# Gates of a gated block in pairs by Strassen's seven half-size products, with low parts of weights by an adding DMA

## The chip, the cores and the metric

The kernel runs on one core of one Trainium2 chip. The metric is the device time of one execution in microseconds (us), lower is better. Engines are named as in the profile: PE (TensorE, matmuls), PEld (its weight loads), DVE (VectorE), ACT (ScalarE), POOL (GpSimd) and SP (the engine that issues most DMAs).

## The reference

One layer over 512 tokens of width 1024, in float32. Of it, these lines matter:

```python
h = rmsnorm(x, norm_mix_pre[l])
(c_q, c_kv, k_r, sg_u, sg_v, cv_x, cv_b, cv_c, pool_in, gate_pre) = split_cols(h @ w_in[l])
gates = jax.nn.sigmoid(gate_pre + gate_b[l]).reshape(B_, S_, N_BRANCH, D_)
y_a = mla(...) @ w_br_mla[l]            # attention branch, (512, 256) @ (256, 1024)
y_b = spatial_gating(...) @ w_br_sg[l]
y_c = short_conv(...) @ w_br_conv[l]
y_d = multiscale_pool(...) @ w_br_pool[l]
merged = (gates[:, :, 0] * y_a + gates[:, :, 1] * y_b
          + gates[:, :, 2] * y_c + gates[:, :, 3] * y_d)
x = x + rmsnorm(merged @ w_out[l], norm_mix_post[l])
h = rmsnorm(x, norm_ffn_pre[l])
f = jnp.square(jax.nn.relu(h @ w_ff1[l])) @ w_ff2[l]     # d_ff = 4096
x = x + rmsnorm(f, norm_ffn_post[l])
```

The four gates are 4 x 1024 columns of `w_in`, so `gate_pre` alone is a product of 512 x 1024 by 1024 x 4096.

## The kernel before

**Three matmuls for one.** Every large product is made from operands split in two: a high part (the value rounded to the format float32r, written by a cast on ACT) and a low part (the value less its high part, written by a subtraction on DVE). `mm3` (line 125) multiplies high by high, high by low and low by high into one PSUM bank. All matmuls go through the wrapper at line 95, so the profile shows L95 for all of PE and ACT; they are told apart by their tiles.

**Weights.** `load` (line 110) brings a tile of 128 x 1024 (512 KB) from HBM into one of three `raw` buffers by a DMA on SP. `split_w` (line 115) casts it to `wh` on ACT and subtracts to `wl` on DVE. `wh` and `wl` have five buffers each. A buffer is written again only when the last matmul that reads it has ended.

**Gates and merge.** The columns are worked in eight blocks b of 128. For each block, `gate(b, i)` (line 439) makes the four gates i = 0 to 3: 24 matmuls (8 K tiles by 3) of 512 columns with the normalized input z, split as `zh` and `zl`, into a bank `fb`; then DVE multiplies the bank by `rbc` into a tile `g`. `merge(b)` (line 447) applies the sigmoid on ACT, loads one tile of branch weights (`wB`), makes four products `y` of 6 matmuls each with the branch results `aT` to `dT`, multiplies each by its gate on DVE, adds them up and splits the sum into `mh` and `ml`. Block 0's gates are made as filler between the steps of attention; the others follow in a loop (lines 669 to 672).

**Output product and feed-forward.** `wo` multiplies the merged tiles by `w_out`, in two halves of columns; each row tile is normalized, added to x (`x1`), transposed (`turn_h`, tiles `tr`) and split into `hh` and `hl`. The first feed-forward product (tiles `z`) starts early for the first four of its 32 hidden row tiles: the lower half of the token columns first (256 columns, line 757), the upper half when the last row tile is there (line 818). The other 28 are made in pairs j, j + 1 by Strassen's scheme (lines 845 to 885): four sums of the quarter weights on DVE, three sums of the halves of h (`hsum`, made once), and seven products `part` of 12 matmuls of 256 columns (4 K tiles by 3) into banks pa to pd, combined by copies on ACT and adds on DVE. `second()` (line 797) makes one K tile of the second product, 12 matmuls of 512 columns into four banks `acc`, from a hidden tile u that `usplit` has split into `uh` and `ul`.

**What sets the order.** PE keeps the program's order. The other engines' instructions are placed by a scheduler when the program is built, and each engine then runs its list strictly in order; waits are semaphores. SP issues its DMAs in order too, each when its buffer is free.

Of the kernel before, what the change touches and what calls it, by code (L numbers as in the profile page):

```python
# [10 lines left out]
F32 = mybir.dt.float32  # L11
# [69 lines left out]
def build(ctx, tc, d, out):  # L81
# [22 lines left out]
    def f(t):  # L104
        return t.bitcast(F32)
# [339 lines left out]
    gates = []  # L445

    def merge(b):
        for i, g in enumerate(gates):
            ACT.activation(g, g, AF.Sigmoid, bias=k1("gateb")[:, i * 8 + b:i * 8 + b + 1])
        w = weights(d["wB"][b])  # L450
        prev = None
        for i, br in ((1, bT), (2, cT), (3, dT), (0, aT)):
            g = gates[i]
# [8 lines left out]
        ACT.copy(mh[:, b, :], prev)  # L462
        DVE.tensor_tensor(ml[:, b, :], prev, f(mh)[:, b, :], ALU.subtract)
        gates.clear()

    others = branches()

# [188 lines left out]
    right = dict(side="right")  # L656

    TOP = 20
    xp = ctx.enter_context(tc.tile_pool(name="xp", bufs=1, reuse_waits="tile", **right))
    x1 = xp.tile([P, NT, D], F32, name="x1")  # L660
    r2 = xp.tile([P, TOP], F32, name="r2")[:, :NT]
    mp = ctx.enter_context(ExitStack())
    mpool = mp.enter_context(tc.tile_pool(name="mp", bufs=1, reuse_waits="tile", **right))
    mh = mpool.tile([P, KD, S], F32R, name="mh")
    ml = mpool.tile([P, KD, S], F32R, name="ml")
    mT = (mh, ml)
    gmix = mpool.tile([P, D], F32, name="gmix")
    gffn = mpool.tile([P, D], F32, name="gffn")
# [4 lines left out]
    nc.sync.dma_start(gmix, d["gmix"].partition_broadcast(P))  # L673
    nc.sync.dma_start(gffn, d["gffn"].partition_broadcast(P))
    for t in range(NT):
        nc.sync.dma_start(x1[:, t, :], d["x"][t * P:(t + 1) * P, :])
    s1.close()

    HK, HS = KD // 2, S // 2
    hs = ExitStack()
    hp_ = hs.enter_context(tc.tile_pool(name="hp", bufs=1, reuse_waits="tile"))

# [41 lines left out]
    for hf in range(2):  # L731
        wo = [weights(d["wO"][hf, c]) for c in range(4)]
        for t in range(NT):
            ps = bank("wo")
            for k in range(KD):
                mm3(ps, sl(mT, slice(None), k, slice(t * P, (t + 1) * P)),
                    sl(wo[k // 2], slice(None), slice((k % 2) * 512, (k % 2 + 1) * 512)), k == 0, k == KD - 1)
# [40 lines left out]
    sst = up.tile([P, 64], F32, name="sst")[:, :4 * NT].rearrange("p (t c) -> p t c", c=4)  # L778
# [50 lines left out]
    A11, A12, A22, S4 = (sl(h2, slice(None), k, t) for k, t in  # L829
                         ((slice(0, HK), slice(0, HS)), (slice(HK, KD), slice(0, HS)), (slice(HK, KD), slice(HS, S)),  # L830
                          (slice(0, HK), slice(HS, S))))
    S1, S2, S3 = (sl(hsum, slice(None), c) for c in range(3))
    fx = hs.enter_context(tc.tile_pool(name="fx", bufs=1, reuse_waits="tile"))
    B1, B2 = slice(0, 512), slice(512, 1024)

    def small():
        return fx.tile([P, HS], F32, tag="x", name="x", bufs=5)

    def part(ps, w, at, a, first):

        for k in range(HK):
            mm3(ps[:, :HS], sl(w, slice(None), slice(at + k * P, at + (k + 1) * P)), sl(a, slice(None), k),
                first and k == 0, k == HK - 1, not first)

    for j in range(EARLY, NFF, 2):
        g, h = u[j], u[j + 1]
        left, rght = load(d["w1"][j]), load(d["w1"][j + 1])
        w = split_w(left)
        w22 = split_w(rght[:, B2], 512)

        DVE.tensor_tensor(left[:, B1], rght[:, B1], left[:, B1], ALU.subtract)
        DVE.tensor_tensor(rght[:, B1], rght[:, B2], rght[:, B1], ALU.subtract)
        DVE.tensor_tensor(rght[:, B2], rght[:, B2], left[:, B1], ALU.subtract)
        DVE.tensor_tensor(left[:, B2], left[:, B2], rght[:, B2], ALU.subtract)
        wl = split_w(left)
        wr = split_w(rght)
        pa, pb = bank("pa"), bank("pb")
        part(pa, w, 0, A11, True)
        x1_ = small()
        ACT.copy(x1_, pa[:, :HS])  # L860
        part(pb, w, 512, A12, True)
        DVE.tensor_tensor(g[:, :HS], pb[:, :HS], x1_, ALU.add)
        pc = bank("pc")
        part(pc, wl, 0, S1, True)
        x5 = small()
        ACT.copy(x5, pc[:, :HS])
        part(pa, wr, 512, S2, False)
        x2 = small()
        ACT.copy(x2, pa[:, :HS])
        pd = bank("pd")  # L870
        part(pd, wl, 512, A22, True)
        second()
        part(pc, w22, 0, S4, False)
        DVE.tensor_tensor(h[:, :HS], pc[:, :HS], x2, ALU.add)
        part(pa, wr, 0, S3, False)
        x3 = small()
        ACT.copy(x3, pa[:, :HS])
        DVE.tensor_tensor(g[:, HS:], pd[:, :HS], x3, ALU.add)  # L878
        DVE.tensor_tensor(h[:, HS:], x3, x5, ALU.add)
# [131 lines left out]
```

## Time and profile before

| | us |
|---|---|
| median of 3 runs (lowest, highest) | 747.95 (746.12, 748.18) |
| the profiled execution: its time | 746.96 |
| the profiled execution: its span in the trace | 745.3 |
| PE busy in the span | 729.6 |
| DVE busy | 470.9 |
| ACT busy | 353.1 |
| POOL busy | 13.3 |

The span is the time from the first to the last traced event of one execution; 1.7 us of the execution's time lie outside it. Matmuls are pipelined: the profile gives one of 512 columns 0.39 us, but the next starts 0.227 us behind it. So a duration of a run of matmuls is read from the chain of work in order of time, which counts from start to start, and not from the busy time of one.

### The profile page before, as it was taken

The numbers are of one execution on the slowest core, as the hardware profiler recorded it, in microseconds if no ns is written. First come the engines' busy times: TensorE is split into PE (matmuls) and PEld (weight loads), VectorE is DVE, ScalarE is ACT, GpSimd is POOL, SyncE is SP. The second block draws the span as 40 slices with busy tenths as digits, with TensorE's granted clock in tenths as the row PEclk, the third lists the DMA queues.
The fourth block names the chain that finished last, engine by engine and source line by source line (L and its number), as shares of the span: only waits on it lengthen the run. The fifth ranks groups of instructions, "written<-read, shape, count | busy, mean of one in ns | idle before, by whom it ended". The sixth has DMA issues, their size and how long they took to land.

```text
span 745.3 us, 10302 instructions
## 1 busy us (share of the span) xinstructions
PE 729.6 (98%) x4058; PEld 637.9 (86%) x4058; DVE 470.9 (63%) x764; ACT 353.1 (47%) x580; POOL 13.3 (2%) x28
## 2 busy tenths in 40 slices
PE   9999999999999999999999699999999999999996
PEld 8988888888888888888889599999999999888885
DVE  7599975366365355455369667776677776774424
ACT  6875543533232323323346356555565556753411
POOL 1110000000000000000000000000000000000001
PEclk9999999999999999999999899999999999999999
DMA  8523231452323223232213014232333233533203
GB/s 306 199 88 114 85 113 58 139 201 85 113 85 98 100 92 107 85 113 86 80 34 113 29 60 142 86 110 86 118 109 111 88 92 133 172 113 104 67 0 113
DMA packets 23152, 78.77 MB, mean 106 GB/s; under 512 B 3008, under 2 KB 3520, under 8 KB 23104
## 3 DMA queue, kind: packets, MB, share of 16 engines
q1 hardware_dynamic: 23072, 78.12, 31.7%
q8 instruction: 32, 0.52, 0.3%
q14 instruction: 16, 0.13, 0.1%
q0 software_dynamic: 32, 0.00, 0.0%
HBM read 76.01 MB, written 2.10 MB: 105 GB/s over the span
## 4 chain that ended last, share of the span: by engine, by line
PE 88%; DVE 8%; ACT 2%; issue 1%; DMA 0%; POOL 0%; SPq 0%; DVEq 0%; ACTq 0%
PE fb L95 26%; PE acc L95 24%; PE pa L95 8%; PE wo L95 6%; PE y L95 6%; PE pc L95 5%; PE psA L95 3%; PE pd L95 3%; PE pb L95 2%; PE z L95 2%; PE sgv L95 2%; DVE wl L119 1%; PE po L95 1%; DVE ql L539 1%; DVE kl L539 1%
## 5 line engine op out<-in xcount | busy, mean ns | idle before, releaser
L95 ACT CAST wh<-raw 128x1024 fp32r<-128x1024 f32 (+2 forms) x154 | 153.9, 1009 | 233.6 <-issue 105.4
L119 DVE TENSOR_TENSOR wl<-raw,wh 128x1024 fp32r<-128x1024 f32 (+2 forms) x154 | 178.7, 1169 | 34.4 <-ACT wh L95 32.3
L95 PE MATMUL fb<-zh,wh 128*128 128x512 f32 x336 | 131.4, 391 | 0.1
L95 PE MATMUL fb<-zh,wl 128*128 128x512 f32 x336 | 130.8, 389 | 0.0
L95 PE MATMUL fb<-zl,wh 128*128 128x512 f32 x336 | 130.8, 389 | 0.0
L95 PE MATMUL acc<-wh,uh 128*128 128x512 f32 x232 | 91.5, 394 | 3.6 <-ACT uh L95 3.6
L95 PE MATMUL acc<-wh,ul 128*128 128x512 f32 x232 | 91.3, 394 | 3.5 <-DVE ul L788 3.5
L95 PE MATMUL acc<-wl,uh 128*128 128x512 f32 x232 | 91.4, 394 | 0.0
L442 DVE TENSOR_TENSOR g<-fb,rbc 128x512 f32<-128x512 f32 x32 | 22.1, 692 | 96.7 <-PE fb L95 96.7
L788 DVE TENSOR_TENSOR ul<-u,uh 128x512 fp32r<-128x512 f32 x58 | 38.7, 690 | 57.3 <-ACT uh L95 57.3
L95 PEld LDWEIGHTS fb<-zh,wl 128*128 128x128 f32 x336 | 63.1, 188 | 13.3
L95 PEld LDWEIGHTS fb<-zh,wh 128*128 128x128 f32 x336 | 63.1, 188 | 13.2 <-DVE zc L351 0.4
L95 PEld LDWEIGHTS fb<-zl,wh 128*128 128x128 f32 x336 | 63.1, 188 | 12.7
L95 PEld LDWEIGHTS acc<-wh,ul 128*128 128x128 f32 x232 | 44.1, 190 | 13.7 <-DVE ul L788 4.3
L95 PEld LDWEIGHTS acc<-wh,uh 128*128 128x128 f32 x232 | 44.0, 190 | 12.5 <-ACT uh L95 4.2
L95 PEld LDWEIGHTS acc<-wl,uh 128*128 128x128 f32 x232 | 44.0, 190 | 8.1
L95 ACT CAST uh<-u 128x512 fp32r<-128x512 f32 x58 | 34.3, 619 | 33.9 <-PE acc L95 33.7
L95 ACT ACTIVATE u<-u 128x512 f32<-128x512 f32 x60 | 33.2, 623 | 15.8 <-DVE u L878 15.8
L95 PE MATMUL pa<-hsh,wh 128*128 128x256 f32 x112 | 31.3, 280 | 0.3 <-ACT x L95 0.3
L95 PE MATMUL pa<-hsl,wh 128*128 128x256 f32 x112 | 31.2, 279 | 0.0
L95 PE MATMUL pa<-hsh,wl 128*128 128x256 f32 x112 | 31.2, 279 | 0.0
L95 PE MATMUL wo<-wh,mh 128*128 128x512 f32 x64 | 25.1, 392 | 0.0
(311 smaller groups left out, 1412.8 us busy)
## 6 DMA issues: line engine op xcount, KB each, us to landing
raw<-in_w SPq DMA_DIRECT2D x64, 512.0 KB, 3.5
raw<-in_wG SPq DMA_DIRECT2D x32, 512.0 KB, 3.4
raw<-in_wF SPq DMA_DIRECT2D x10, 512.0 KB, 3.5
raw<-in_wB SPq DMA_DIRECT2D x8, 512.0 KB, 3.4
raw<-in_wO SPq DMA_DIRECT2D x8, 512.0 KB, 3.4
xk<-in_x SPq DMA_DIRECT2D x4, 512.0 KB, 8.8
x<-in_x SPq DMA_DIRECT2D x4, 512.0 KB, 5.9
out<-f SPq DMA_DIRECT2D x8, 256.0 KB, 2.0
```

The source lines that it names most:

```text
L95: ins = op(*a, **k)
L119: DVE.tensor_tensor(lo[:, :n], raw[:, :n], f(hi)[:, :n], ALU.subtract)
L442: DVE.tensor_tensor(g, ps, rbc, ALU.mult)
L539: DVE.tensor_tensor(dst[1][rows, :], src, f(dst[0])[rows, :], ALU.subtract)
L788: DVE.tensor_tensor(ul, u[j], f(uh), ALU.subtract)
```

## The change

1. **Blocks 2 to 7.** The gates are made in pairs (0, 1) and (2, 3), each by `seven`, the code that was in the feed-forward loop, now a generator. z takes the place of h: three sums of its quarters (`zsum`) are made once while the gates of blocks 0 and 1 run, and a quarter of `zh` and `zl` is overwritten with a fourth sum. The results are multiplied by `rbc` in SBUF.
2. **The merge** is a generator too. The merge of block b - 1 is put into the first pair of block b, one product y behind each of the parts 2, 3, 5 and 6. Block 7's merge stands alone.
3. **`split_by_dma`** makes the low part without DVE: ACT writes the high part, then its negative into `wl`, and a DMA on POOL's queue adds the raw weights from HBM to it. It is used for the raw parts of the gate pairs (w and w22), for all merges and for the first four feed-forward tiles. The sums of weights (wl and wr) are still split by `split_w`.
4. **`second()`** is first called behind the upper halves of all four early tiles (it was called behind the second), and once more inside the first pair.
5. **Memory.** The merged tiles are single tiles in two pools. x1, gmix and gffn are allocated, and their loads issued, behind the merges.

```diff
+    def split_by_dma(src, raw=None, n=1024):
+        raw = load(src, n) if raw is None else raw
+        hi = wp.tile([P, 1024], F32R, tag="wh", name="wh", bufs=5)
+        lo = wp.tile([P, 1024], F32R, tag="wl", name="wl", bufs=5)
+        ACT.copy(hi[:, :n], raw[:, :n])
+        ACT.activation(lo[:, :n], f(hi)[:, :n], AF.Copy, scale=-1.0)
+        POOL.dma_start(lo[:, :n], src.bitcast(F32R), accum_op=ALU.add)
         return hi, lo
...
+    def seven(srcs, forms, small, g, h, by_dma):
+        A11, A12, A22, S1, S2, S3, S4 = forms
+        left, rght = load(srcs[0]), load(srcs[1])
+        if by_dma:
+            w = split_by_dma(srcs[0], left)
+            w22 = split_by_dma(srcs[1][:, B2], rght[:, B2], 512)
+        else:
+            w = split_w(left)
+            w22 = split_w(rght[:, B2], 512)
+        DVE.tensor_tensor(left[:, B1], rght[:, B1], left[:, B1], ALU.subtract)
...
+        wl = split_w(left)
+        wr = split_w(rght)
+        pa, pb = bank("pa"), bank("pb")
+        part(pa, w, 0, A11, True)
+        x1 = small()
+        ACT.copy(x1, pa[:, :HS])
+        yield
+        part(pb, w, 512, A12, True)
+        DVE.tensor_tensor(g[:, :HS], pb[:, :HS], x1, ALU.add)
+        yield
...
     def merge(b):
-        for i, g in enumerate(gates):
+        gs = list(gates)
+        gates.clear()
+        for i, g in enumerate(gs):
             ACT.activation(g, g, AF.Sigmoid, bias=k1("gateb")[:, i * 8 + b:i * 8 + b + 1])
-        w = weights(d["wB"][b])
+        w = split_by_dma(d["wB"][b])
...
+            yield
...
-    for b in range(KD):
-        while len(gates) < 4:
-            gates.append(gate(b, len(gates)))
-        merge(b)
...
+    ops = forms(z, zsum)
+    for b in range(2, KD):
+        steps = merge(b - 1)
+        for i in (0, 2):
+            g, h = (gp.tile([P, S], F32, tag="g", name="g", bufs=6) for _ in range(2))
+            for n, _ in enumerate(seven((d["wG"][4 * b + i], d["wG"][4 * b + i + 1]), ops, small_g, g, h, True)):
+                if i == 0 and n in (1, 2, 4, 5):
+                    next(steps)
+                if i == 0 and n == 5:
+                    rest(steps)
+            for x in (g, h):
+                DVE.tensor_tensor(x, x, rbc, ALU.mult)
+            gates.extend((g, h))
+    rest(merge(KD - 1))
...
-        w, ps = weights(d["w1"][j]), bank("z")
+        w, ps = split_by_dma(d["w1"][j]), bank("z")
...
+        if j == EARLY - 1:
+            second()
         pend.append((j, usplit(j)))
-        if j:
-            second()
```

In the rows of the order below, a number behind a name tells one buffer's use from the next, a bracket names the semaphores that the instruction waits for (DMASW are DMAs of POOL's queue, DMAHW those of SP's), and L95 is the wrapper's line.

ACT, the cast of a merge's weights. Before, in block 1 (wh_2197 is the merge's, the others are gates' weights, g the sigmoids):

```order
L95 CAST wh_2127<-raw_2125 128x1024 [waits DMAHW2_49,PE_49,Activation_49]
L95 ACTIVATE g_1977<-g_1977,c1_109 128x512 [waits DVE_49]
L95 CAST wh_2160<-raw_2158 128x1024 [waits DMAHW3_49,PE_49,Activation_49]
L95 ACTIVATE g_2010<-g_2010,c1_109 128x512 [waits DVE_49]
L95 CAST wh_2197<-raw_2195 128x1024 [waits DMAHW4_49,PE_49,Activation_49]
```

Now, where block 3 begins (wh_2217 and wh_2221 are the sums of its first pair, wh_2260 the merge's of block 2; pa_2095 is the last product of block 2's second pair, pa_2225 the first of block 3):

```order
L95 CAST wh_2217<-raw_2199 128x1024 [waits DVE_49,PE_49]
L95 CAST wh_2221<-raw_2201 128x1024 [waits PE_49]
L95 CAST wh_2260<-raw_2258 128x1024 [waits DMAHW3_49,PE_49]
L95 COPY x_2191<-pa_2095 128x256 [waits PE_49]
L95 ACTIVATE wl_2261<-wh_2260 128x1024 [waits DMASW4_49,Activation_49]
L95 COPY x_2239<-pa_2225 128x256 [waits PE_49]
```

The cast of wh_2197 waited for the last product y of the merge before; that of wh_2260 waits for the last matmul but one of pa_2095, the last that reads the high part of the sums of the pair before. Behind it now stand a copy, the negated copy, and on POOL the adding DMA.

PE, the first product y of a merge. Before, in block 1, behind the last gate (fb):

```order
L95 MATMUL fb_2164<-zl_105,wh_2160 128x512
L95 MATMUL fb_2164<-zh_104,wl_2161 128x512
L95 MATMUL y_2201<-bh_112,wh_2197 128x512 [waits DVE_49,Activation_49]
L95 MATMUL y_2201<-bl_113,wh_2197 128x512
L95 MATMUL y_2201<-bh_112,wl_2198 128x512 [waits DVE_49]
```

Now, in block 3, behind the second part (pb) of its first pair:

```order
L95 MATMUL pb_2226<-zl_105,wh_2203 128x256
L95 MATMUL pb_2226<-zh_104,wl_2204 128x256
L95 MATMUL y_2265<-ah_110,wh_2260 128x512 [waits Activation_49]
L95 MATMUL y_2265<-al_111,wh_2260 128x512
L95 MATMUL y_2265<-ah_110,wl_2261 128x512 [waits DMASW1_49]
```

The third matmul of the merge waited for DVE's subtraction and now waits for a DMA of POOL's queue, 24 matmuls of 256 columns and two of 512 behind the end of the pair before.

PE, the first K tile of the second product (acc). Before, it stands behind the upper half of early tile 1:

```order
L95 MATMUL z_3373<-hl_2968,wh_3369 128x256
L95 MATMUL z_3373<-hh_2967,wl_3370 128x256
L95 MATMUL acc_3531<-wh_3603,uh_3567 128x512 [waits PE_49,Activation_49]
L95 MATMUL acc_3531<-wl_3604,uh_3567 128x512
L95 MATMUL acc_3531<-wh_3603,ul_3568 128x512 [waits DVE_49]
```

Now behind that of early tile 3:

```order
L95 MATMUL z_4298<-hl_3799,wh_4293 128x256
L95 MATMUL z_4298<-hh_3798,wl_4294 128x256
L95 MATMUL acc_4375<-wh_4503,uh_4411 128x512 [waits PE_49,Activation_49]
L95 MATMUL acc_4375<-wl_4504,uh_4411 128x512
L95 MATMUL acc_4375<-wh_4503,ul_4412 128x512 [waits DVE_49]
```

Two more upper halves, 48 matmuls, stand ahead of it. And on ACT, ahead of them, the negated copies of early tiles 2 and 3 (wh_4241, wh_4293) stand behind work on the last row tiles of the output product:

```order
L95 CAST hh_3798<-tr2_4156 128x4x128 [waits PE_49]
L95 ACTIVATE sq_4165,stt_3814<-x1_3792 128x1024 [waits DVE_49,Activation_49,Pool_49]
L95 COPY lower_3815<-tr2_4149 128x4x128 [waits DVE_49]
L95 COPY lower_3815<-tr2_4156 128x4x128 [waits DVE_49]
L95 ACTIVATE wl_4242<-wh_4241 128x1024 [waits DMASW6_49]
L95 ACTIVATE sq_4287,stt_3814<-x1_3792 128x1024 [waits DVE_49,DMAHW5_49,Activation_49,Pool_49]
L95 ACTIVATE wl_4294<-wh_4293 128x1024 [waits DMASW4_49]
```

Before, no such copy was there: the low parts were subtractions in DVE's list, behind the same copies' sources.

## Rows read from the trace of the kernel before

**Rows 1.** The page's busy times, and its chain by engine (shares of span).

```profile
PE 729.6 (98%) x4058; PEld 637.9 (86%) x4058; DVE 470.9 (63%) x764; ACT 353.1 (47%) x580; POOL 13.3 (2%) x28
...
PE 88%; DVE 8%; ACT 2%; issue 1%; DMA 0%; POOL 0%; SPq 0%; DVEq 0%; ACTq 0%
```

**Rows 2.** Chain in time, one block: start us, duration us, engine, tile, matmuls.

```profile
183.26 21.76 PE fb L95 x96
205.02 5.44 PE y L95 x24
```

**Rows 3.** The same chain in the first feed-forward product, part of one pair.

```profile
520.71 2.75 PE acc L95 x12
523.46 1.40 PE pa L95 x12
```

**Rows 4.** Stretches: length; busy of PE, PEld, DVE, ACT, POOL; clock; DMA share, GB/s.

```profile
178.00:341.00 163.00, 163.00 (x721) 134.97 (x720) 84.14 (x102) 50.09 (x61) 0.00 (x0) 1.00 0.30 97
```

**Rows 5.** Groups on ACT and DVE by shape: busy us, mean ns | idle before.

```profile
L95 ACT CAST wh<-raw 128x1024 fp32r<-128x1024 f32 x138 | 144.1, 1053 | 211.7 <-issue 105.4 <-PE pc L95 42.1 <-PE fb L95 40.6
L95 ACT COPY x<-pa 128x256 f32<-128x256 f32 x42 | 15.5, 369 | 4.3 <-PE pa L95 3.2
L119 DVE TENSOR_TENSOR wl<-raw,wh 128x1024 fp32r<-128x1024 f32 x138 | 167.7, 1223 | 27.3 <-ACT wh L95 25.3 <-issue 0.3
L852 DVE TENSOR_TENSOR raw<-raw 128x512 f32<-128x512 f32 x14 | 9.7, 692 | 0.5
L862 DVE TENSOR_TENSOR u<-pb,x 128x256 f32<-128x256 f32 x14 | 5.9, 420 | 2.1 <-PE pb L95 2.1
```

**Rows 6.** DMA issues: tile, queue, count, KB each, median us to landing.

```profile
raw<-in_wB SPq DMA_DIRECT2D x8, 512.0 KB, 3.4
x<-in_x SPq DMA_DIRECT2D x4, 512.0 KB, 5.9
gmix<-in_gmix SPq DMA_DIRECT2D x1, 512.0 KB, 4.9
gffn<-in_gffn SPq DMA_DIRECT2D x1, 512.0 KB, 5.8
pos<-in_pos POOLq DMA_DIRECT2D x1, 2.0 KB, 2.6
```

**Rows 7.** Chain in time, start of the feed-forward.

```profile
392.67 8.49 PE z L95 x72
401.15 0.45 PE tr L95 x4
...
417.58 0.61 DVE ul L788
...
433.82 1.40 PE pa L95 x12
```

**Rows 8.** PE in time there: start, duration, [idle before, its releaser].

```profile
414.04 0.50 PE L95 MATMUL acc<-wh,uh 128*128 128x512 f32 x1 [3.60 <-ACT uh L95]
...
418.24 0.80 PE L95 MATMUL acc<-wh,ul 128*128 128x512 f32 x1 [3.47 <-DVE ul L788]
```

**Rows 9.** Stretches there; the number behind POOL's is the granted clock.

```profile
415.00:416.00 1.00, 0.00 (x0) 0.00 (x0) 1.00 (x3) 0.00 (x0) 0.00 (x0) 0.76 0.00 0
420.00:422.00 2.00, 2.00 (x6) 1.52 (x6) 0.12 (x1) 0.00 (x0) 0.00 (x0) 0.50 0.00 0
422.00:424.00 2.00, 2.00 (x16) 1.86 (x15) 0.00 (x0) 0.00 (x0) 0.00 (x0) 0.91 0.00 0
```

**Rows 10.** Stretches at the end of the kernel.

```profile
738.00:740.00 2.00, 0.85 (x4) 0.38 (x2) 0.24 (x2) 0.78 (x2) 0.00 (x0) 1.00 0.70 262
742.00:744.00 2.00, 0.00 (x0) 0.00 (x0) 0.05 (x1) 0.00 (x0) 0.00 (x0) 0.80 0.70 262
```

**Rows 11.** ACT in time, end of the output product.

```profile
395.05 1.19 ACT L95 COPY lower<-tr 128x512 f32<-128x512 f32 x2 [0.46 <-DVE hl L721]
```

**Rows 12.** The stretch from attention's tail into block 1.

```profile
90.00:178.00 88.00, 87.95 (x454) 74.28 (x452) 50.25 (x97) 36.78 (x70) 0.20 (x2) 1.00 0.35 120
```

More of the change, by code (lines that the diff above doesn't have):

```diff
@@ L306, in build, with part, forms @@
     s2.close()
+    HK, HS = KD // 2, S // 2
+    B1, B2 = slice(0, 512), slice(512, 1024)
+    def part(ps, w, at, a, first):
+        for k in range(HK):
+            mm3(ps[:, :HS], sl(w, slice(None), slice(at + k * P, at + (k + 1) * P)), sl(a, slice(None), k),
+                first and k == 0, k == HK - 1, not first)
+    def seven(srcs, forms, small, g, h, by_dma):
[8 more added lines that the diff above has]
+        DVE.tensor_tensor(left[:, B1], rght[:, B1], left[:, B1], ALU.subtract)
+        DVE.tensor_tensor(rght[:, B1], rght[:, B2], rght[:, B1], ALU.subtract)
+        DVE.tensor_tensor(rght[:, B2], rght[:, B2], left[:, B1], ALU.subtract)
+        DVE.tensor_tensor(left[:, B2], left[:, B2], rght[:, B2], ALU.subtract)
+        wl = split_w(left)
[8 more added lines that the diff above has]
+        yield
+        pc = bank("pc")
+        part(pc, wl, 0, S1, True)
+        x5 = small()
+        ACT.copy(x5, pc[:, :HS])
+        yield
+        part(pa, wr, 512, S2, False)
+        x2 = small()
+        ACT.copy(x2, pa[:, :HS])
+        yield
+        pd = bank("pd")
+        part(pd, wl, 512, A22, True)
+        yield
+        part(pc, w22, 0, S4, False)
+        DVE.tensor_tensor(h[:, :HS], pc[:, :HS], x2, ALU.add)
+        yield
+        part(pa, wr, 0, S3, False)
+        x3 = small()
+        ACT.copy(x3, pa[:, :HS])
+        DVE.tensor_tensor(g[:, HS:], pd[:, :HS], x3, ALU.add)
+        DVE.tensor_tensor(h[:, HS:], x3, x5, ALU.add)
+        yield
+    def forms(x, sums):
+        lo, hi, t0, t1 = slice(0, HK), slice(HK, KD), slice(0, HS), slice(HS, S)
+        return [sl(x, slice(None), k, t) for k, t in ((lo, t0), (hi, t0), (hi, t1))] + [
+            sl(sums, slice(None), c) for c in range(3)] + [sl(x, slice(None), lo, t1)]
     s3 = ExitStack()
@@ L447, in merge @@
     def merge(b):
-        for i, g in enumerate(gates):
+        gs = list(gates)
+        gates.clear()
+        for i, g in enumerate(gs):
             ACT.activation(g, g, AF.Sigmoid, bias=k1("gateb")[:, i * 8 + b:i * 8 + b + 1])
-        w = weights(d["wB"][b])
+        w = split_by_dma(d["wB"][b])
         prev = None
-        for i, br in ((1, bT), (2, cT), (3, dT), (0, aT)):
-            g = gates[i]
+        for i, br in ((1, bT), (2, cT), (3, dT), (0, aT)) if b == 0 else enumerate((aT, bT, cT, dT)):
+            g = gs[i]
             ps = bank("y")
@@ L461, in merge @@
             prev = g
-        ACT.copy(mh[:, b, :], prev)
-        DVE.tensor_tensor(ml[:, b, :], prev, f(mh)[:, b, :], ALU.subtract)
-        gates.clear()
+            yield
+        ACT.copy(mT[0][b], prev)
+        DVE.tensor_tensor(mT[1][b], prev, f(mT[0][b]), ALU.subtract)
     others = branches()
@@ L658, in build @@
     TOP = 20
-    xp = ctx.enter_context(tc.tile_pool(name="xp", bufs=1, reuse_waits="tile", **right))
-    x1 = xp.tile([P, NT, D], F32, name="x1")
[L661 to L667, printed above, removed]
@@ L668, in build, with merged @@
-    gffn = mpool.tile([P, D], F32, name="gffn")
-    for b in range(KD):
-        while len(gates) < 4:
-            gates.append(gate(b, len(gates)))
-        merge(b)
[L673 to L686, printed above, removed]
+    mp = ctx.enter_context(ExitStack())
+    mT = [], []
+    def merged(name, pad):
+        pool = mp.enter_context(tc.tile_pool(name=name, bufs=1, reuse_waits="tile", **right))
+        for b in range(HK):
+            for c in range(2):
+                mT[c].append(pool.tile([P, S], F32R, name=f"m{'hl'[c]}{len(mT[c])}"))
+        if pad:
+            pool.tile([P, TOP], F32, name="top")
@@ new lines, in build, with small_g, rest @@
+    merged("mp0", True)
+    s4 = ExitStack()
+    ss = s4.enter_context(tc.tile_pool(name="ss", bufs=1, reuse_waits="tile"))
+    ss.tile([P, 8], F32, name="shift")
+    zsum = [ss.tile([P, 3, HK, HS], F32R, name=f"zs{c}") for c in "hl"]
+    def small_g():
+        return ss.tile([P, HS], F32, tag="x", name="x", bufs=5)
+    def rest(steps):
+        for _ in steps:
+            pass
+    while len(gates) < 4:
+        gates.append(gate(0, len(gates)))
+    tq = ExitStack()
+    tqp = tq.enter_context(tc.tile_pool(name="tq", bufs=1, reuse_waits="tile", **right))
@@ new lines, in build, with z_sums @@
+    lower = []
+    def z_sums(hh):
+        q = tqp.tile([P, 4, 2, HS], F32, name=f"q{hh}")
+        a11, a12, a21, a22 = (q[:, c] for c in range(4))
+        for c, (k, t) in enumerate(((0, 0), (HK, 0), (0, HS), (HK, HS))):
+            ix = slice(None), slice(k + 2 * hh, k + 2 * hh + 2), slice(t, t + HS)
+            DVE.tensor_tensor(q[:, c], f(zh)[ix], f(zl)[ix], ALU.add)
+        DVE.tensor_tensor(a22, a21, a22, ALU.add)
+        DVE.tensor_tensor(a21, a11, a21, ALU.subtract)
+        DVE.tensor_tensor(a11, a22, a11, ALU.subtract)
+        DVE.tensor_tensor(a12, a12, a11, ALU.subtract)
+        for c, v in enumerate((a22, a11, a21)):
+            ix = slice(None), c, slice(2 * hh, 2 * hh + 2)
+            ACT.copy(zsum[0][ix], v)
+            DVE.tensor_tensor(zsum[1][ix], v, f(zsum[0])[ix], ALU.subtract)
+        lower.append(a12)
@@ new lines, in build @@
+    steps = merge(0)
+    for i in range(4):
+        next(steps)
+    rest(steps)
+    for i in range(4):
+        gates.append(gate(1, i))
+        if i % 2 == 0:
+            z_sums(i // 2)
+    for hh, v in enumerate(lower):
+        ix = slice(None), slice(2 * hh, 2 * hh + 2), slice(HS, S)
+        ACT.copy(zh[ix], v)
+        DVE.tensor_tensor(zl[ix], v, f(zh)[ix], ALU.subtract)
+    tq.close()
+    merged("mp1", False)
+    ops = forms(z, zsum)
[5 more added lines that the diff above has]
+                if i == 0 and n in (1, 2, 4, 5):
+                    next(steps)
+                if i == 0 and n == 5:
+                    rest(steps)
+            for x in (g, h):
+                DVE.tensor_tensor(x, x, rbc, ALU.mult)
+            gates.extend((g, h))
@@ L687, in build @@
+    rest(merge(KD - 1))
+    s4.close()
+    s1.close()
+    xp = ctx.enter_context(tc.tile_pool(name="xp", bufs=1, reuse_waits="tile"))
+    x1 = xp.tile([P, NT, D], F32, name="x1")
+    r2 = xp.tile([P, lines(NT)], F32, name="r2")[:, :NT]
     hs = ExitStack()
@@ L696, in build @@
     wk_ = ws.enter_context(tc.tile_pool(name="wk", bufs=1, reuse_waits="tile"))
+    gmix = wk_.tile([P, D], F32, name="gmix")
+    gffn = wk_.tile([P, D], F32, name="gffn")
+    nc.sync.dma_start(gmix, d["gmix"].partition_broadcast(P))
+    nc.sync.dma_start(gffn, d["gffn"].partition_broadcast(P))
+    for t in range(NT):
+        nc.sync.dma_start(x1[:, t, :], d["x"][t * P:(t + 1) * P, :])
     yg = wk_.tile([P, NT, D], F32, name="yg")
@@ L735, in build @@
             for k in range(KD):
-                mm3(ps, sl(mT, slice(None), k, slice(t * P, (t + 1) * P)),
+                mm3(ps, sl([m[k] for m in mT], slice(None), slice(t * P, (t + 1) * P)),
                     sl(wo[k // 2], slice(None), slice((k % 2) * 512, (k % 2 + 1) * 512)), k == 0, k == KD - 1)
@@ L837, in small @@
         return fx.tile([P, HS], F32, tag="x", name="x", bufs=5)
[L839 to L843, printed above, removed]
+    ops = forms(h2, hsum)
     for j in range(EARLY, NFF, 2):
         g, h = u[j], u[j + 1]
[L847 to L879, printed above, removed]
@@ L880, in build @@
+        for n, _ in enumerate(seven((d["w1"][j], d["w1"][j + 1]), ops, small, g, h, False)):
+            if n == 4 or n == 1 and j == EARLY:
+                second()
         while pend:
```

8 lines of the change are left out of this document (2 added, 6 removed).

## The prediction

> **What bounds the kernel now.** I began with the page's busy shares: TensorE (PE) is busy for 98% of the span, no other engine for more than 63% [rows 1]. The chain of work that ended last says the same: 88% of it is PE [rows 1]. So a matmul saved is time saved, where nothing else then arrives late. The next view is that chain in order of time. A block of gates is 96 matmuls of 512 columns in 21.76 us and the merge behind it 24 in 5.44 us, back to back [rows 2]: 27.20 us a block, 0.227 us a matmul. The first feed-forward product already uses the seven half-size products, and there 12 matmuls of 256 columns take 1.40 us, again back to back [rows 3]. The table by stretches confirms it: PE is busy for the whole of 178 to 341 us, while DVE and ACT have 79 and 113 us to spare there [rows 4]. The one place where PE stands still is the start of the first feed-forward product: waits of 3.60 and 3.47 us for the split of the first hidden rows [rows 8], and then matmuls at half the granted clock [rows 9].
>
> **Term 1, the seven products.** A pair of gates costs 21.76 / 2 = 10.88 us today and 7 x 1.40 = 9.80 us after: 1.08 us less. Blocks 2 to 7 hold twelve pairs: **-13.0 us**. The new side work goes on engines with room. In DVE, a block loses five low parts of 1.22 us (four gates, one merge) and gains eight sums of 0.69, four low parts of 1.22 and eight combinations of 0.42 [rows 5]: from 84.14 / 6 = 14.0 to about 21.7 us, against 25.0 us of PE work (two pairs and a merge). ACT goes from 50.09 / 6 = 8.3 to about 19 us (each pair: three casts of 1.05 and one of half the size, two negated copies of like sizes, four copies of 0.37). Both stay below PE, so I cost them at nothing; were the low parts of the raw weights not moved from DVE to the DMA, its sum would be 21.7 + 2 x (1.22 + 0.69) + 1.22 = 26.7 us and it would be the bound (0.69 from the sum of the same size).
>
> **Term 2, the merge's weights.** Here the change adds a wait. Before, every block made five splits in a ring of five buffers, so a merge's weights reused the buffer of the merge a block earlier, were cast a block ahead and cost PE nothing. Now a block makes nine splits in the same five buffers. The order shows that the cast of the merge's weights (wh_2260) stands right ahead of the copy of the last product of the pair before, and both wait for that product: the buffer is the one that this product reads last. From the end of that pair the chain is: cast 1.05, the copy queued behind it 0.37, the negated copy about 1.05 (the nearest row is the cast of the same size) [rows 5], together 2.5 us; then the adding DMA on the POOL queue, D. PE meanwhile has two products, 2 x 1.40, and the two matmuls that need only the high part, 2 x 0.227, together 3.25 us; its third matmul of the merge reads the low part. So PE waits 2.5 + D - 3.25 = D - 0.75. Queued behind PE's wait is everything else of the block; nothing overtakes it. The POOL queue holds only such DMAs there, and those ahead of this one wait for older work.
>
> D is not in the trace. A lone plain load of the same 512 KB takes 3.4 us; the only DMA that POOL issues takes 2.6 us for 2 KB; two loads issued together (gmix, gffn) take 4.9 and 5.8, four together 5.9 at the median [rows 6]. The adding DMA also reads its destination, and the merge's cast frees a load buffer, so that SP issues two loads of 512 KB about 1.4 us ahead of it. I take 5.3, the middle of the two loads issued together, which is the nearest case; ends 3.4 and, for twice a lone load, 6.8. That gives a wait of 4.55 us (2.65 to 6.05). The Trainium skill, page "DMA: Bandwidth & Descriptors", section "Anatomy of one DMA — SWDGE (gpsimd) path", fits a DMA issued by GpSimd as 2.0 us plus bytes over 436 GB/s, which by that page would be an estimated 3.2 us here and a wait of 2.45 us; it says nothing of an add, and no run here shows one.
>
> The wait also touches the clock. In the rows the granted clock was 1.00 while PE had stood still from 410.4 us but for two matmuls, fell to 0.50 after 415 us, and came back in 422 to 424, four microseconds after PE resumed [rows 8, 9]; at the kernel's end it falls inside 742 to 744, PE having stopped before 739 [rows 10]. From 418.24 to about 422.4 PE ran at half speed and lost 2.1 us. A wait of 4.55 us is at the edge of this, so I add half, 1.0 (ends 0 and 2.1). Six merges (blocks 1 to 6, inside the first pairs of blocks 2 to 7) have it; block 7's merge reuses a buffer free for long, and block 0's is loaded during attention. 6 x 5.55 = **+33.3 us**. Each block is then 25.0 + 5.55 = 30.6 us instead of 27.2.
>
> **Term 3, the start of the feed-forward.** From the first early product (392.67) to the first pair (433.82) pass 41.15 us [rows 7]. PE's work in it is eight halves of 2.80, a transposition of 0.87 and three K tiles of the second product at 2.75: 31.5 us; 9.6 us are waiting and half clock. Now all four upper halves stand ahead of the first K tile, which gives DVE 5.6 us more time. But two low parts come late by the DMA: in the third early product, the negated copy stands behind the copies that end at 396.24 today [rows 11]; 396.24 + 1.05 + 5.3 = 402.6, and PE would want it at 392.67 + 5.60 + 0.23 = 398.5: a wait of 4.1. The transposition moves behind it to 406.0 at its end, and DVE's chain from there to the first low part of u takes 418.2 - 401.6 = 16.6 us today [rows 7], 0.5 less with one split halved: 422.1. PE gets there at 406.0 + 2.80 + 11.2 + 0.45 = 420.5: a wait of 1.6. With 0.3 for the next pair, which exists today too, 6.0 us of the 9.6 remain: **-3.6 us** (D of 3.4: -5.5; D of 6.8: -1.6).
>
> **Term 4, the rest.** The sums of z are 22 operations of 0.69, 15 us of DVE, between 90 and 178 us, where DVE idles for 38 of 88 us [rows 12]. They are hidden unless one stands ahead of a softmax step: 0, at most +3. x, gmix and gffn are loaded later; the 21.8 us of the first half of the output product cover gmix, so 0.
>
> **Sum.** The profiled execution took 746.96 us, 1.0 below the median of 747.95. 746.96 - 13.0 + 33.3 - 3.6 = **763.7 us**, 2% slower.
>
> **Rivals.** *A short DMA* (the other side). If the add costs no more than a plain load, D is 3.4, PE waits 2.65 and the clock holds: 746.96 - 13.0 + 15.9 - 5.5 = 744.4. For it: a lone load is that fast. Against: two loads are ahead and the destination is read as well. The break-even is a loss of about 2.9 us per merge, D near 3.7. By the Trainium skill's fit above it would be an estimated 743. *Break-even:* D near 4, wait 3.25, no clock loss: 746.96 - 13.0 + 19.5 - 4.9 = 748.6. *A long DMA:* D of 6.8 and the clock falling each time: 6 x 8.15 = 48.9, so 746.96 - 13.0 + 48.9 - 1.6 = 781.3; beyond it, the pair's own low part, issued 2.5 us into the pair before and wanted 9.8 + 0.2 us into it, is late too from D = 7.5 on. *The products do not do what they say:* with 1.55 us instead of 1.40 a pair saves nothing, and the sum is 776.7. Against it speaks [rows 3], the same shapes with other work between them.
>
> **Chances.** Forecast (755 to 775) 0.45; long DMA 0.20; products without gain 0.05; break-even 0.15; short DMA 0.15. A measurement of this kernel tells about 0.3%, some 2.2 us, from no change. Faster by more than that 0.15, within it 0.15, slower 0.70. The range leaves out about one in ten on each side: 743 (short DMA) to 785 (long DMA, with the 3 us of term 4).
>
> **What would show it.** In blocks 2 to 7: matmuls pa to pd at 1.40 us per twelve; one PE wait per block, at the third matmul of y<-ah, released by the adding DMA, 4 to 5 us long; blocks of 30 us. The DMA list gives D: near 5 the forecast stands, near 3.4 the kernel is level or faster. A granted clock below 1.00 behind those waits shows the clock's part. At the feed-forward: a wait in the third early product for the DMA, a short one before the first acc, and no half clock. The forecast is wrong if PE shows no wait at y, or waits elsewhere (for DVE sums, or in attention).

## The result and the profile after

The changed kernel takes 793.82 us (median; 791.31 to 794.88) against 748.07 us before: a ratio of 1.061, 95% interval 1.060 to 1.063. It is 6% slower; the forecast was 2% slower, and the time lies beyond the range's upper end of 785. The profiled execution took 794.88 us, its span is 793.2 us (before: 745.3).

The page of the kernel after: busy us and share of the span by engine, and the chain that ended last by engine. These answer to [rows 1].

```profile
PE 737.3 (93%) x4490; PEld 662.1 (83%) x4490; DVE 517.1 (65%) x872; ACT 421.1 (53%) x696; POOL 43.6 (5%) x64
...
PE 72%; DVE 10%; DMA 8%; issue 5%; ACT 3%; POOL 0%; DVEq 0%; POOLq 0%; ACTq 0%
```

PE's busy time grew by 8 us although it has fewer columns to multiply, and it now stands still for some 7% of the span. In the chain, transfers have 8% where they had 0%. The list of PE's waits says where (tile waited with and its releaser: total us, times, longest):

```profile
PE y L95 <- DMA wl<-in_wB: 41.3, 7, 8.0
PE z L95 <- DMA wl<-in_w: 2.6, 1, 2.6
PE wo L95 <- ACT mh L95: 1.5, 1, 1.5
```

41.1 of the 41.3 us are six waits in blocks 2 to 7, each at the third matmul of the merge. In PE's rows in time (start, duration, [idle before, its releaser]) the first, the second and the last of the six are:

```profile
186.64 0.80 PE L95 MATMUL y<-ah,wl 128*128 128x512 f32 x1 [4.66 <-DMA wl<-in_wB]
222.22 0.79 PE L95 MATMUL y<-ah,wl 128*128 128x512 f32 x1 [7.18 <-DMA wl<-in_wB]
363.01 0.80 PE L95 MATMUL y<-ah,wl 128*128 128x512 f32 x1 [8.01 <-DMA wl<-in_wB]
```

The chain in order of time around the second one, where [rows 2] had only matmuls back to back:

```profile
209.78 1.43 PE pa L95 x12
...
211.24 2.43 issue
...
213.69 8.49 DMA wl<-in_wB
...
222.22 2.07 PE y L95 x4
```

The pair before ends at 211.2, the adding DMA begins 2.5 us later and lasts 8.49 us, and PE waits for it. Then four merge matmuls take 2.07 us, where four take 0.91 at full clock (24 in 5.44 [rows 2]). The stretches there show why (length; busy of PE, PEld, DVE, ACT, POOL; granted clock; DMA share, GB/s), as in [rows 9]:

```profile
216.00:218.00 2.00, 0.00 (x0) 0.00 (x0) 0.00 (x0) 1.58 (x2) 0.10 (x1) 1.00 0.85 250
218.00:220.00 2.00, 0.00 (x0) 0.00 (x0) 1.33 (x2) 0.00 (x0) 0.76 (x1) 0.66 0.99 248
220.00:222.00 2.00, 0.00 (x0) 0.00 (x0) 0.05 (x1) 0.00 (x0) 0.00 (x0) 0.50 1.12 221
222.00:224.00 2.00, 1.77 (x4) 1.49 (x5) 0.00 (x0) 0.00 (x0) 0.00 (x0) 0.50 0.67 133
224.00:226.00 2.00, 2.00 (x12) 1.90 (x12) 0.69 (x1) 0.00 (x0) 0.00 (x0) 0.63 0.02 4
226.00:228.00 2.00, 2.00 (x14) 1.74 (x13) 0.29 (x1) 0.38 (x1) 0.00 (x0) 1.00 0.00 0
```

The granted clock falls to its lower level, half, while PE stands still, and stays there for some 3 us after PE has resumed. The page's DMA issues (tile, queue, count, KB, median us to landing) give the price that [rows 6] did not have:

```profile
raw<-in_wG SPq DMA_DIRECT2D x32, 512.0 KB, 3.6
wl<-in_wG POOLq DMA_DIRECT2D x12, 512.0 KB, 7.0
...
raw<-in_wB SPq DMA_DIRECT2D x8, 512.0 KB, 4.4
wl<-in_wB POOLq DMA_DIRECT2D x8, 512.0 KB, 8.1
...
wl<-in_wG POOLq DMA_DIRECT2D x12, 256.0 KB, 4.0
```

Where the 47.9 us of span come from is read from the first starts of the tiles. The long stretch runs from the end of block 1's gates to the output product. Before, it begins with block 1's merge (two pieces of the chain); after, with the first product of block 2, because that merge now stands inside the block (first and last start of two tiles):

```profile
177.82 5.44 PE y L95 x24
...
346.46 32.64 PE wo L95 x144
```

```profile
L95 PE MATMUL pa<-zh,wh x48: 278/283/283, 178.5 to 379.0; 128*128 128x256 f32 x48
...
L95 PE MATMUL wo<-wh,mh x64: 389/389/496, 393.9 to 440.6; 128*128 128x512 f32 x64
```

That is 215.4 us instead of 168.6 (+46.8). Ahead of it there are 0.8 more; from the output product to the first early tile 48.1 instead of 46.1 (+2.0); from there to the feed-forward's last pair 248.3 instead of 250.1 (-1.8); the rest is level.

### The profile page after: what moved, and what is told of

It reads as the page before. It is cut to its first block, busy times and chain, and to the rows that moved or that the text cites. A ratio compares the mean times of both kernels' runs of the same rounds, so it can differ in the third digit from the quotient of the medians.

```text
span 793.2 us, 11529 instructions
## 1 busy us (share of the span) xinstructions
PE 737.3 (93%) x4490; PEld 662.1 (83%) x4490; DVE 517.1 (65%) x872; ACT 421.1 (53%) x696; POOL 43.6 (5%) x64
## 4 chain that ended last, share of the span: by engine, by line
PE 72%; DVE 10%; DMA 8%; issue 5%; ACT 3%; POOL 0%; DVEq 0%; POOLq 0%; ACTq 0%
PE acc L95 21%; PE pa L95 11%; PE pc L95 9%; PE fb L95 6%; DMA wl<-in_wB 6%; PE y L95 5%; PE pd L95 4%; PE wo L95 4%; PE pb L95 3%; PE psA L95 3%; DVE wl L119 2%; PE sgv L95 1%; ACT wh L95 1%; PE z L95 1%; DMA wl<-in_w 1%
## 5 line engine op out<-in xcount | busy, mean ns | idle before, releaser
L95 ACT CAST wh<-raw 128x1024 fp32r<-128x1024 f32 (+2 forms) x178 | 173.3, 985 | 138.1 <-PE pc L95 55.0
L119 DVE TENSOR_TENSOR wl<-raw,wh 128x1024 fp32r<-128x1024 f32 (+2 forms) x142 | 163.9, 1164 | 34.8 <-ACT wh L95 26.9
L95 PE MATMUL acc<-wh,ul 128*128 128x512 f32 x232 | 90.5, 390 | 1.1 <-DVE ul L932 1.1
L95 PE MATMUL acc<-wh,uh 128*128 128x512 f32 x232 | 90.7, 391 | 0.0
L95 PE MATMUL acc<-wl,uh 128*128 128x512 f32 x232 | 90.6, 391 | 0.0
L95 PE MATMUL fb<-zh,wh 128*128 128x512 f32 x144 | 56.7, 394 | 0.1
L95 PE MATMUL fb<-zl,wh 128*128 128x512 f32 x144 | 56.1, 390 | 0.0
L95 PE MATMUL fb<-zh,wl 128*128 128x512 f32 x144 | 56.1, 390 | 0.0
L95 PEld LDWEIGHTS acc<-wh,ul 128*128 128x128 f32 x232 | 43.6, 188 | 11.2 <-DVE ul L932 1.9
L540 DVE TENSOR_TENSOR g<-g,y 128x512 f32<-128x512 f32 x32 | 21.7, 684 | 47.8 <-PE y L95 47.8
L95 ACT CAST uh<-u 128x512 fp32r<-128x512 f32 x58 | 34.3, 618 | 34.2 <-PE acc L95 33.7
L95 PEld LDWEIGHTS acc<-wh,uh 128*128 128x128 f32 x232 | 43.6, 188 | 8.6 <-ACT uh L95 0.4
L95 PEld LDWEIGHTS acc<-wl,uh 128*128 128x128 f32 x232 | 43.6, 188 | 7.9
L95 PE MATMUL y<-ah,wl 128*128 128x512 f32 x16 | 10.2, 638 | 41.3 <-DMA wl<-in_wB 41.3
L95 PEld LDWEIGHTS y<-ah,wl 128*128 128x128 f32 x16 | 4.5, 279 | 45.1 <-DMA wl<-in_wB 44.4
L95 ACT ACTIVATE u<-u 128x512 f32<-128x512 f32 x60 | 33.2, 622 | 16.5 <-DVE u L377 16.5
L95 ACT COPY x<-pa 128x256 f32<-128x256 f32 x78 | 28.5, 366 | 20.3 <-PE pa L95 18.6
L95 ACT COPY x<-pc 128x256 f32<-128x256 f32 x26 | 9.4, 363 | 53.9 <-PE pc L95 53.9
L95 ACT ACTIVATE wl<-wh 128x1024 fp32r<-128x1024 f32 (+1 forms) x36 | 32.9, 915 | 0.5
L95 PE MATMUL pa<-hsh,wh 128*128 128x256 f32 x112 | 31.3, 280 | 0.7 <-ACT x L95 0.7
L95 PEld LDWEIGHTS fb<-zh,wl 128*128 128x128 f32 x144 | 27.0, 188 | 5.8
```

The costliest lines, as they stand in the source:

```text
L95: ins = op(*a, **k)
```

## Experiments

Times are medians, each beside runs of the kernel before on the same chip (747.3 us for the first eight kernels, 748.0 for the last). "Merge" is the product y with the weights of wB, "pairs" the seven products, "early tiles" the first four of the feed-forward.

| kernel | us | ratio to before, 95% interval |
|---|---|---|
| changed, merge on DVE | 736.2 | 0.985 (0.983 to 0.987) |
| changed, merge's weights in their own buffer | 742.7 | 0.994 (0.993 to 0.996) |
| changed, merge's transfer without adding | 782.1 | one run |
| before, merge by adding DMA | 747.9 | one run |
| before, merge by plain copy on the software queue | 747.9 | one run |
| before, second product later | 739.8 | 0.990 (0.988 to 0.991) |
| changed, no adding DMA in the blocks | 760.5 | 1.018 (1.016 to 1.019) |
| changed, merge and early tiles on DVE | 731.3 | 0.978 (0.976 to 0.980) |
| the same, z moved by 32 bytes | 732.6 | 0.980 (0.979 to 0.982) |

**The merge's low part on DVE again.**

```diff
-        w = split_by_dma(d["wB"][b])
+        w = weights(d["wB"][b])
```

> Changed kernel with one edit: the low part of the merge's weights (blocks 1 to 7 and 0) is subtracted on DVE again; the pairs' w and w22 keep the adding DMA and the merge keeps its ring buffer and its place. Theory A (the six waits of 41.1 us are the adding DMA, which has to begin after product 7 of the pair before has freed the buffer, and PE's low clock follows from those waits): the chain becomes cast 1.05 plus subtraction 1.23 instead of 2.5 plus about 8, which is under the 3.25 us that PE has, so the six waits fall under 0.5 us each and the granted clock of blocks 2 to 7 goes back to 1.00; the time is 793.8 less 41.1 less some 15 to 18 of clock, 735 to 739 us. Theory C (the clock falls because products and merge steps are interleaved in this way, waits or not): waits vanish, clock stays near 0.88, some 750 us. Theory D (the buffer is simply free too late, whoever writes it; DVE works in order and comes late): waits of 1 to 3 us each stay, 745 to 760 us.

Measured 736.2 us. PE's longest wait is now this one, and none is at y; the granted clock over blocks 2 to 7 is 1.00, and the chain there is matmuls alone:

```profile
PE z L95 <- DMA wl<-in_w: 3.3, 1, 3.3
```

```profile
210.89 1.40 PE pa L95 x12
212.29 1.44 PE pd L95 x12
213.73 1.39 PE y L95 x6
215.12 1.43 PE pc L95 x12
```

So the six waits and the low clock come with the transfer, and interleaving by itself costs no clock: theories C and D fall. The stretch from block 2 to the output product is 158.7 us:

```profile
L95 PE MATMUL pa<-zh,wh x48: 278/283/283, 178.2 to 322.5; 128*128 128x256 f32 x48
...
L95 PE MATMUL wo<-wh,mh x64: 389/389/477, 336.9 to 381.7; 128*128 128x512 f32 x64
```

Against the 215.4 of the changed kernel this is 56.7 us: 41.1 of waits and 15.6 behind them, 2.6 per wait in the mean.

**A buffer of its own for the merge, split half a block ahead, still by the adding DMA.**

```diff
+    mw = [ss.tile([P, 1024], F32R, name=f"mw{c}") for c in "hl"]
...
         for i in (0, 2):
+            if i == 2:
+                wm = merge_weights(b)
```

> Changed kernel with one edit: the merge's weights of blocks 1 to 7 have a buffer of their own and are split, still by the adding DMA, half a block ahead (before the second pair of the block before). Theory A (late start behind a late buffer): the same transfer of about 8 us has some 20 us of cover, the y waits are 0. What is late next: the ring now gets 8 splits a block, so the first pair's w takes the buffer that the pair of 9.8 us before it has freed only at its start: 2.5 plus 8.1 against 9.8, a wait of some 0.6 to 1 us at the first product of each block, perhaps with some of the clock; 737 to 745 us. Theory B (the adding DMAs are slow because they are queued behind each other, whichever buffer): transfers of 8 us stay and grow where three follow each other, waits move to pa, over 755 us. Theory C (clock falls without waits): about 750 us.

Measured 742.7 us. The same transfer is there, nobody waits for it at y, and the next one in line shows, as expected:

```profile
PE pa L95 <- DMA wl<-in_wG: 4.5, 5, 1.8
```

```profile
mwl<-in_wB POOLq DMA_DIRECT2D x7, 512.0 KB, 7.2
```

At 7.2 us the transfer is free when it starts early enough: what made it dear is the buffer that came free last. Five waits of 4.5 us in all cost 7.1 us in the stretch (165.8 against 158.7), which again is more than their length.

**What the transfer is made of: three kernels.** The adding DMA in the changed kernel against a plain copy in its place, and both again in the kernel before, where no other such DMA runs.

```diff
-        POOL.dma_start(lo[:, :n], src.bitcast(F32R), accum_op=ALU.add)
+        POOL.dma_start(lo[:, :n], src.bitcast(F32R))
```

> Changed kernel, but the merge's low-part DMA of blocks 1 to 6 copies the raw weights over the buffer instead of adding them (same queue, same place, same 512 KB, no accumulation; so the low part of those weights is left wrong and the copy stands for the transfer alone). Theory A1 (the length of 8 us is the price of adding): the transfer falls to the 3.6 to 4.4 us of the plain raw loads, the six waits from 6.9 to about 3.5 us in the mean, the time to some 765 to 772 us. Theory B (the length is the software queue and the traffic of the pair's own transfers beside it): it stays at 7 to 8.5 us, 788 to 794 us.

> Kernel before with one edit: the merge's low parts come by the adding DMA, all else is as before (no pairs, no adding DMA for the gates; the ring of five then gives the merge a buffer that has been free for about a block). The price of one adding DMA with no other one near it. Theory A1 (adding itself is slow): 6.5 to 8 us for 512 KB. Theory B (slow only because the pair's adding DMAs and raw loads run beside it): 3.4 to 5 us. In either case nobody waits for it for long: 746 to 750 us.

> Kernel before, with the merge's low parts by a plain copy on the software queue (the same transfer as the adding one put into the kernel before, without accumulation; the low parts of the merge's weights are left wrong). The fourth corner: adding took 6.6 us in quiet and 7.8 to 8.8 us in the changed kernel, the plain copy 6.0 to 7.1 us there. If adding costs about 1.8 us wherever it is, the plain copy takes 4.6 to 5 us in quiet; if the software queue alone makes it slow, 6 us or more; if it is as fast as the same bytes on SP's queue, 3.4 us, and then traffic costs a plain copy some 2.8 us but an adding one only 1.5. Time as before, 746 to 750 us.

Of the kernel with the plain copy, the transfer's pieces of the chain in blocks 3 and 7, and then the same two of the changed kernel:

```profile
211.32 6.04 DMA wl<-in_wB
...
345.56 6.86 DMA wl<-in_wB
```

```profile
213.69 8.49 DMA wl<-in_wB
...
354.14 8.82 DMA wl<-in_wB
```

In the kernel before, adding and then plain (one row of each kernel's DMA issues):

```profile
wl<-in_wB POOLq DMA_DIRECT2D x8, 512.0 KB, 6.6
```

```profile
wl<-in_wB POOLq DMA_DIRECT2D x8, 512.0 KB, 4.3
```

512 KB take 3.4 us on SP's queue [rows 6], 4.3 on POOL's queue (the software queue of the page) and 6.6 when they are added, with nothing else of the kind near (medians of eight). In the changed kernel the plain copy takes 6.5 us and the adding one 8.3 (means of the last five blocks). So each theory had a part: the queue 0.9, adding 1.7 to 2.3, traffic 1.7 to 2.2 us. The adding DMA also holds the transfer engines longer, 1.9 times as long per byte by the queues of the changed kernel's page (SP's, then the software queue: packets, MB, share of 16 engines' span).

```profile
q1 hardware_dynamic: 23072, 78.12, 29.9%
q0 software_dynamic: 5216, 15.73, 11.4%
```

Most of that is the adding. In the kernel before, the same bytes take 1.7 times as much on the software queue when they are added as in a plain copy (the queue's row with adding, then without):

```profile
q0 software_dynamic: 1184, 4.20, 3.4%
```

```profile
q0 software_dynamic: 1184, 4.20, 2.0%
```

Without adding, the waits were 31.0 us instead of 41.3 and the time still 782 us; the add alone does not explain the loss. I had expected 765 to 772 or 788 and more, and it fell between. Its stretch from block 2 to the output product is 205.3 us, 46.6 over the version with the merge on DVE: 31.0 of these waits, 1.3 of waits at pa, and 14.3 behind them. Shorter waits lost nearly as much clock.

**The second product later, alone.**

```diff
+        if j == EARLY - 1:
+            second()
         pend.append((j, usplit(j)))
-        if j:
-            second()
...
+        if j == EARLY:
+            second()
```

> Kernel before with one edit: the second product of the first four K tiles is put later, as in the change (one of them ahead of the last early tile's split, the others in the first pair); no pairs in the gates, no adding DMA. The size of term 3 by itself. The prediction has minus 3.6 us. In the changed kernel's trace the stretch from the first early tile to the first pair is 7.9 us shorter and the pairs are 6.1 us longer, which is minus 1.8 net, though there the early tiles' low parts came by DMA, with a wait of 2.6 us for one of them. Theory A: the order alone is worth minus 3 to minus 4 us, and the transfer ate part of it. Theory B: the waits of 3.6 and 3.5 us only move to the first pair (pa behind its x), so it is worth minus 1 to minus 2.

Measured 739.8 us, minus 7.5: twice what I gave the order, and a miss on both theories. PE's one wait in the start of the feed-forward, and the stretch in which it falls, with the clock at 1.00 where [rows 9] had 0.50 behind the waits:

```profile
PE acc L95 <- DVE ul L788: 1.2, 1, 1.2
```

```profile
416.00:418.00 2.00, 0.80 (x5) 0.35 (x4) 2.00 (x4) 1.34 (x3) 0.00 (x0) 1.00 0.00 0
```

**No adding DMA in the blocks at all.**

```diff
-        w = split_by_dma(d["wB"][b])
+        w = weights(d["wB"][b])
...
-... ops, small_g, g, h, True)):
+... ops, small_g, g, h, False)):
```

> Changed kernel without any adding DMA in the blocks: the merge's and the pairs' low parts are all subtracted on DVE. With the merge alone on DVE, DVE is busy 133.7 of 162 us in blocks 2 to 7 (21.9 us a block of 25.5) and the first products take 1.43 to 1.44 us per 12 matmuls, where the feed-forward's same products take 1.40. The edit puts two subtractions of 1.22 and two of 0.69 us on DVE, 3.8 us a block: 25.7 us against PE's 25.5. Theory A (DVE becomes the bound): PE waits for wl or for g, 0.5 to 2 us a block with some of the clock, 739 to 750 us. Theory E (the 0.03 to 0.04 us per product come from the transfers beside it, and DVE just keeps up): products at 1.40, block at 25.0, 733 to 735 us.

Measured 760.5 us, 24 us over the version with only the merge on DVE. PE waits for DVE:

```profile
PE y L95 <- DVE wl L119: 12.8, 5, 2.6
PE y L95 <- ACT wh L95: 2.5, 5, 0.5
```

It lies beyond both theories. The chain ahead of one of these waits shows DVE's list, in which the merge's low part (the second of the two rows wl) is last:

```profile
207.93 1.14 DVE wl L119
209.06 0.34 DVE g L357
209.40 1.14 DVE wl L119
...
210.58 1.45 PE y L95 x4
212.03 2.56 PE pc L95 x12
```

DVE is busy for 152.9 of 188 us in this stretch, 81%. So it is not full, though theory A and the prediction's 26.7 us a block had made it the bound: it is late at one place in each of five blocks, and 15.3 us of waits with the half clock behind them (12 matmuls in 2.56 us) become 25.5. The clock falls behind these waits for DVE as it does behind those for the DMA, so it goes with the wait and not with what ends it. The adding DMA is thus worth having in the pairs, where it has a pair's time as cover.

**The early tiles' low parts on DVE too.**

```diff
-        w, ps = split_by_dma(d["w1"][j]), bank("z")
+        w, ps = weights(d["w1"][j]), bank("z")
```

> The version with the merge on DVE, with one more edit: the four early tiles' low parts are subtracted on DVE too, so the wait of 3.3 us for the transfer at the third early tile has no transfer left. Theory A: that wait goes, and DVE has room (it is busy 26.2 of 48 us ahead of it): minus 2 to minus 3, 733 to 735 us. Theory B: the four subtractions of 1.22 us stand in DVE's list ahead of the sums hsl that set the start of the pairs, the start comes no earlier: 736 to 740 us.

Measured 731.3 us, 5.0 less than with the merge alone on DVE, where 3.3 was the wait, and more than theory A's 2 to 3. In the changed kernel's chain the transfer and the matmuls behind it are

```profile
440.18 7.75 DMA wl<-in_w
447.96 8.45 PE z L95 x46
```

The wait is at the third matmul of the second early tile, for 46 matmuls stand between it and the last transposition, and before, 72 of three tiles did [rows 7]; the expectation has it at the third. The 46 take 8.45 us where they take 5.4 at full clock (72 in 8.49 [rows 7]). The last transposition, DVE's sums and the first pair all come later by that wait and its clock. This version beats both kernels.

**z moved by 32 bytes.**

```diff
+    zp.tile([P, 8], F32, name="shift_z")
     zh = zp.tile([P, KD, S], F32R, name="zh")
     zl = zp.tile([P, KD, S], F32R, name="zl")
+    zp.tile([P, 24], F32, name="pad_z")
```

> The version with the merge and the early tiles on DVE, with one more edit: the tiles zh and zl lie 32 bytes further on in each partition (a pad of 32 bytes ahead of them and one of 96 behind, so that nothing else changes its place within 128 bytes). Of the seven products of a pair four read z and take 1.43 to 1.44 us, three read the sums zs and take 1.40, as do all seven in the feed-forward. zs and the feed-forward's hh lie 32 bytes past a multiple of 64, zh, zl and the weights on one. Theory F (the moving tile's place against the weights' is what costs): the four take 1.40 too, 48 products by 0.035 to 0.04 are 1.7 to 1.9 us, 729 to 730 us; more if the single gates' 128x512 matmuls gain as well. Theory G (it is the interleaving with the merge, or the transfers beside it): they stay at 1.43 to 1.44, 731 us.

The product on A12, by its matmuls (busy us, mean ns), without the shift and then with it:

```profile
L95 PE MATMUL pb<-zl,wh 128*128 128x256 f32 x48 | 13.6, 283 | 0.0
```

```profile
L95 PE MATMUL pb<-zl,wh 128*128 128x256 f32 x48 | 13.4, 279 | 0.0
```

In the chain these products go from 1.44 to 1.40 us per 12, so theory F holds for them. But the stretch from block 2 to the output product takes 158.4 us, only 0.3 less than with the merge alone on DVE, where no wait stands in it either: the products on the sums and the merge, whose places did not change against the weights, take about 0.01 us more each, and no run shows why. The single gates' 96 matmuls of 512 columns, in blocks 0 and 1, go the other way, from 21.76 to 22.40 us, and the whole is level with the version without the shift (intervals overlap).

## Why the prediction was wrong, point by point

| term | predicted | measured |
|---|---|---|
| 1, seven products | -13.0 | -9.9 |
| 2, merge's weights | +33.3 | +56.7 |
| 3, start of the feed-forward | -3.6 | -1.8 |
| 4, the rest | 0 | +2.8 |

745.3 - 9.9 + 56.7 - 1.8 + 2.8 = 793.1, against a span of 793.2 us.

**Term 2: mechanism, place and formula right, two sizes wrong.** It is short by 23.4 us, 13.8 in the waits (27.3 forecast, 41.1 measured) and 9.6 in the clock (6.0 and 15.6). The buffer of the last product, 2.5 us of chain, the third matmul of the merge, six times: all as written. The wait follows D - 0.75: a D of 5.23 in block 2 would give 4.48 (4.66 measured), 8.49 gives 7.74 (7.18), 8.82 gives 8.07 (8.01). The step that failed is the choice of D: "the middle of the two loads issued together", 5.3, with ends of 3.4 and 6.8. All those rows were plain loads on SP's queue. The step named the destination's being read and the loads ahead, but counted them inside those ends; measured, the queue, the add and the traffic come on top of each other, 8.3 us in five of the six blocks. Even in quiet it is 6.6, near my upper end. By the Trainium skill, page "DMA: Bandwidth & Descriptors", section "Anatomy of one DMA — SWDGE (gpsimd) path", 512 KB would be an estimated 3.2 us; the plain copy measured 4.3 in quiet and 6.5 in traffic, so the trace does not agree here, and the add is outside that fit.

The other size is the clock: I took 1.0 per wait with an end of 2.1, and 2.6 was lost in the mean, by the difference of two kernels. Read from the chain it is 1.8 to 3.1, and not in the order of the waits' lengths: behind 4.66 us, the shortest, four matmuls of y took 2.08 us and 12 of pc 2.56, where 0.91 and 1.42 are due; behind 7.18 us less was lost. The price that [rows 8, 9] showed once (2.1) was to be taken whole. The rivals that let the clock hold behind 2.65 and 3.25 us had the same error: behind the 2.6 at z it fell. The rival "long DMA" (781.3, at 0.20) had the right case. The profiled execution lies 13.6 us past it: 4.8 for the longer waits, 3.0 for the clock, and the rest from terms 1 and 4 (3.1 and 2.8).

**Term 1: right in kind, 3.1 us too large.** 168.6 us became 158.7 where no wait is left. A product on z takes 1.43 to 1.44, not the 1.40 of [rows 3]: four of seven products read z, 48 in all, some 1.8 us; the products on the sums take up to 1.42, some 0.3 over 36; and the split merge takes 1.39 per six matmuls instead of 1.36, 0.7 over 24. That [rows 3] had "the same shapes" was not enough; where the tile lies counted too, as the shift shows.

**Term 3: two errors that half cancel.** The order alone is worth -7.5, not the -5.5 that the shorter transfer would have left: with the upper halves ahead, a wait of 1.2 us remains and the clock never falls. The early tiles' adding DMA gave back 5.0 (the difference of two versions). My forecast had waits of 4.1 us at the third early tile, 1.6 at the first acc and 0.3 at the first pair, 6.0 in all; measured are 2.6 at the second early tile, 1.1 and 0.7, which is 1.6 less. But it expected no half clock there, and that took some 3.0 behind the first of them. That -3.6 came near -1.8 is in part luck.

**Term 4: small, and partly open.** Ahead of block 2 there are 0.8 us more; five versions with the same sums of z have 0.2 to 0.6 there, so not all of it is shown to be theirs. The output product takes 2.0 more, 1.5 of it a wait for mh. That wait isn't in the lists of the versions with the merge on DVE or with its own buffer (46.3 and 46.5 us there); with the plain copy, as late, it is 1.1. So it comes with the late start and not with the adding; what is delayed in between, no run separates.

## What to carry to other kernels

A transfer that takes work off an engine has a latency, and what counts is when its buffer comes free: count the allocations of one round against the ring, and see which product frees the one that is needed first. An adding DMA of 512 KB here needs some 11 us of cover from the moment that its buffer comes free, cast and negated copy included; where a pair's time covers it, it was worth 24 us, where it did not, it cost 58. Price a wait of PE at its length plus the clock it loses, and price an operation that no row shows above the nearest plain one, not between plain ones.

## What the runs showed of the hardware

- 512 KB into SBUF: 3.4 us on SP's queue, 4.3 on POOL's, 6.6 with accumulation, and 6.5 and 8.3 for the latter two beside this kernel's other transfers; 256 KB with accumulation take 4.0.
- Per byte the adding transfers held the transfer engines 1.9 times as long as plain ones on SP's queue, and 1.7 times as long as plain ones on their own.
- Behind six PE waits of 4.7 to 8.0 us, matmuls at the lower clock lost 1.8 to 3.1 us each time; behind one of 2.6 us they lost some 3.0.
- 12 matmuls of 256 columns take 1.40 us with the moving tile 32 bytes past a multiple of 64 and the weights on one, and 1.43 to 1.44 with both on one; with 512 columns 96 took 22.40 and 21.76, the reverse.
